# Weaving two kinds of recurrent chains into projections: fixed waits against an estimate of the engines' queues

## The chip, the cores and the metric

The kernel runs on one core of a Trainium2 chip. The core has a matmul engine (PE), a vector engine (DVE), an activation engine (ACT), a general engine (POOL), and a queue (SP) that starts transfers. Each takes its instructions in the order in which they stand in its queue. The metric is the device time of one launch in microseconds (us), the median of several runs.

## The reference, cut to what matters

One layer of a decoder with 2048 prompt tokens, 16 meta tokens and 8 short sample sequences of 4 tokens. The normalised tokens go through one input projection. Four heads are retention heads, four are gated delta-rule heads; both are recurrences over chunks of 128 tokens. Then come the output projection, a norm, a dense feed-forward part and a second norm.

```python
proj = h @ w_in
# retention, per chunk c of 128 tokens
scores = (q @ k.T) * decay
out    = scores @ v + q_d @ s
s      = gamma**C * s + k_d.T @ v
# gated delta rule, per chunk
lower  = strict_tril(k @ k.T * decay) * beta
w_v, w_k = solve(I + lower, [v * beta, k * beta * gam])
u      = w_v - w_k @ s
out    = q_g @ s + (q @ k.T * decay) @ u
s      = cd * s + k_t.T @ u
# after either: out = rms_norm(out) * silu(gate)
y = layer_norm(alpha * h + concat(out_r, out_g) @ w_out);  y = layer_norm(alpha * y + swiglu(y))
```

## The kernel before

**Stages.** The first stage, `attention`, takes the tokens in four blocks of four chunks (block 0 has a fifth, short tile with the sample and meta tokens). `attn_block` goes through the eight heads of a block in the order of `order(b)`, retention (r) and delta rule (g) mixed: r0 g0 r1 g1 r2 g2 r3 g3, and in the last block r0 g0 g1 r1 g2 g3 r2 r3. The second stage is the output projection and the feed-forward part; it is not touched.

**Projections.** `ret_proj` and `gdn_proj` compute a head's projections. float32 operands are split in two float32r parts, so each product is three matmuls (`mm3`, line 288). The results go to PSUM tiles `pj`. The weights arrive by transfer as `raw` and are split into `wh` (ACT, line 237) and `wl` (DVE, line 244). In `ret_proj` DVE writes `qk` and `rotB` (lines 439 and 440, the rotary step) and `rg` (line 456). Both functions are generators: `mm3g` yields after each few products.

**Chains.** When a head's projections are written, its chain is started, and runs beside the projections of the heads after it. `ret_chain` is the retention: `flip` (turn q and k), `score`, `mix` for each chunk, then the norm, and a turn of each output (line 563, `rt` from `rv`). `gdn_chain` runs `gdn_group` for the four chunks of a block together (and in block 0 a second, small group for the short tile). Its steps are: decays E by `mg` (line 788); turned values and keys, `vb` (805, 806) and `kT` (810, 812); the products kT x kT (816); LT, the masked product (818); the inverse of I + LT by block doubling, which starts with the factors `Z` and `U` (827, 828), then `T` (834, products of U with the unit matrix), six levels in which `w` from `T` and `Lm` gives `Z` (840, 842) and `w` from `Z` and `U` gives the next T and U (847, 849); a refinement; and then the recurrence, chunk after chunk: products with the state S (902, 903), `r` (905), `u` (910, 911), and the new S and output V (919 to 922). `Lm`, the masks of the six levels, are six instructions on POOL (830). At the end come the sums of squares, a reciprocal square root by some twelve small DVE instructions on tiles `rqa`, `rqt`, `rqy` (lines 189 to 201), the multiplication of V by it (929, 931), four turns on PE (933, `sc` from `ident` and V), and a product with the gate (937). A delta-rule chain must be over before the next one starts (`start` calls `finish`).

**The order of the work.** The program is written by one Python loop: it takes the next piece of a projection, and then asks `advance` whether a chain may issue its next step. Before, each `yield` of a chain names a fixed wait out of a table (`LAT`, 17 numbers), times a factor (`SLACK`), and `advance` subtracts the projection work that has been written:

```
38   LAT = [1.0, 0.7, 0.7, 0.7, 2.0, 0.7, 0.5, 1.2, 1.8, 0.9, 1.0, 1.0, 1.7, 1.0, 0.6, 0.5, 0.5]
974      def advance(self, us):
975          for key in list(self.active):
976              c = self.active[key]
977              c[1] -= us
978              while c[1] <= 0:
979                  w = next(c[0], None)
980                  if w is None:
981                      del self.active[key]
982                      break
983                  c[1] += w * SLACK[key]
```

What is written is then ordered once more by a scheduler: it gives each engine's queue its order, and lets a ready instruction pass one that is not ready, earlier written ones first. So the order on the engines is read from the built program, not from the code alone.

Of the kernel before, what the change touches and what calls it, by code (L numbers as in the profile page):

```python
# [148 lines left out]
class _Cut:  # L149
    """Allocates [128, full, ...] tiles and hands out their first n rows of dim 1."""  # L150
# [13 lines left out]

class Builder:
    def __init__(self, tc, I, O):
        self.tc, self.nc, self.I, self.O = tc, tc.nc, I, O
        _, self.off, self.gam, _ = _consts()
        self.es = ExitStack()
# [13 lines left out]
    def rsqrt(self, x, n, rows, pool, scale, eps):  # L183
        """(scale x + eps)^-0.5; x may be a list of equal parts."""
# [19 lines left out]
    def layer_norm(self, src, rows, g, b, pool, fast=False, pinned=False):  # L204
        """LayerNorm of rows in place; src is the row, or its two halves. fast: the vector engine alone."""
# [42 lines left out]
    def load_piece(self, src, ab=False, ring=None, later=False, el="dve"):  # L248
        """2048 (+64) columns of weights as a pair of float32r parts."""
# [26 lines left out]
    def mm3g(self, out, lh, ll, rh, rl, kn, per):  # L276
        """As mm3, with a yield of the tensor engine's time after every few k."""
# [6 lines left out]
    def mm3(self, out, lh, ll, rh, rl, kn, first=True, last=True):  # L284
        """out (+)= sum_k l(k)^T r(k), with float32 operands in two float32r parts."""
# [55 lines left out]
    def phase_ln(self, b):  # L341
        """Embedding LayerNorm of the tokens of block b, a tile at a time."""
# [11 lines left out]
    def first_block(self):  # L354
        """As phase_ln and turned for the first block, whose tokens and weights are loaded together."""
# [38 lines left out]
    def phase_t(self, b, tiles, x=None):  # L394
        """Transposes of normalised rows, one tile of tokens at a time."""
# [14 lines left out]
    def next_piece(self):  # L410
        """The weights whose turn it is; the load of those after them starts."""
        w = self.ahead
        while self.pend:
            self.split(*self.pend.pop(0))
        self.age = 0
        self.ahead = self.load_piece(*self.todo.pop(0), later=True) if self.todo else None
        return w

    def ret_proj(self, b, h, gates, out, before=None):
# [39 lines left out]
        if before and b == 0:  # L459
            # the weights come before the tokens: each tile of these meets all of those  # L460
# [20 lines left out]
    def ret_chain(self, b, h, qkvg, mixd):  # L481
        """The retention itself; yields the time until its next products can start."""
# [62 lines left out]

        flip(0)
        yield LAT[0]
        for t in range(n):
            score(t)
            yield LAT[1]  # L550
            if t + 1 < n:
                flip(t + 1)
                yield LAT[2]
            mix(t)
            yield LAT[3]
        rs = self.rsqrt(ss[:, :n], n, 128, self.sm, 4.0 / HD, 4.0 * RMS_EPS)
        yield LAT[4]
        for t, (rows, c0, ch) in enumerate(tiles):
            orow = NS if ch < 0 else 128
            o = oc[t]  # L560
            nc.vector.scalar_tensor_tensor(out=o, in0=o, scalar=rs[:orow, t:t + 1], in1=vg[t][1][:orow], op0=ALU.mult, op1=ALU.mult)
            p = self.prt.tile([128, 128], F32, tag="rt", name="rt")[:, :orow]
# [5 lines left out]
            yield LAT[5]  # L568
# [3 lines left out]
    def state_out(self, kt, u, S0, cd, gam, out):  # L572
        """out_b = decay_b S0_b + kt_b^T u_b for the eight sample sequences."""
# [82 lines left out]
    def gdn_proj(self, b, h, G, out):  # L656
# [15 lines left out]
        def flip(a):  # L672
            """Token-major q or k: sums of squares, and k itself."""
# [73 lines left out]
    def gdn_chain(self, b, h, cvz, G, mixd):  # L747
        """The gated delta rule itself; yields as ret_chain does."""
# [16 lines left out]
    def gdn_group(self, b, h, cv, zg, sk, kp, G, mixd, ts, tiles):  # L765
        """One group of chunks; yields where the tensor engine has to wait for another one."""
# [16 lines left out]
        # decays exp(G_i - G_j) as [j, i]  # L783
# [466 lines left out]
```

## Time and profile before

| | |
|---|---|
| device time, median of 3 runs | 3137.73 us (3137.69 to 3143.98) |
| the profiled execution: from its first to its last instruction | 3141.4 us |
| PE busy | 2994.8 us, 95% |
| DVE busy | 1826.4 us, 58% |
| ACT, POOL busy | 967.1 us, 565.9 us |
| end of the first stage | about 1366 us |

In a row of the profile, the line number is that of the code before; `pj<-wh,xT` names the tile written and the tiles read. A matmul with float32 operands is recorded as two. "Idle" ahead of an instruction is put down to what it waited for last. The granted clock is PE's clock as a share of full speed.

### The profile page before, as it was taken

How to read it: one execution, taken by the hardware profiler on the slowest of the kernel's cores; microseconds unless marked ns; L12 is line 12 of the kernel's file. 1: busy time of each engine (PE TensorE's matmuls, PEld its weight loads, DVE VectorE, ACT ScalarE, POOL GpSimd, SP SyncE). 2: the span in 40 equal slices, each digit the busy share in tenths (PEclk: the TensorE clock that was granted, in tenths of full speed). 3: DMA queues.
4: the chain of work that ended last, by engine and by line, in shares of the span. 5: the costliest groups of instructions: out<-in, count | busy, mean ns of one | idle time of the engine just before them, and what ended most of it. 6: DMA issues, size and time to landing. Idle time of an engine off the chain costs nothing. (4 is left out here: it accounts for less than half of the span.)

```text
span 3141.4 us, 44842 instructions
## 1 busy us (share of the span) xinstructions
PE 2994.8 (95%) x17858; PEld 2593.6 (83%) x17858; DVE 1826.4 (58%) x4024; ACT 967.1 (31%) x2179; POOL 565.9 (18%) x570
## 2 busy tenths in 40 slices
PE   7999998999999988999999999999999999999997
PEld 6988887888888877878999999998777877878787
DVE  7777777877787777767333333333684343333346
ACT  2434443545544545433111111111233111111111
POOL 1332222221222122202100001110131000001002
PEclk9999998999999999999999999999999999999999
DMA  5222222222222111152111111112242111111111
GB/s 198 85 75 79 95 99 79 88 93 88 78 93 97 59 53 66 48 180 64 54 41 54 41 41 54 41 41 68 71 145 81 41 54 41 54 41 54 40 41 54
DMA packets 91986, 225.28 MB, mean 72 GB/s; under 512 B 10960, under 2 KB 39168, under 8 KB 91776
## 3 DMA queue, kind: packets, MB, share of 16 engines
q1 hardware_dynamic: 91776, 222.41, 21.5%
q8 instruction: 140, 2.29, 0.3%
q14 instruction: 70, 0.57, 0.1%
HBM read 191.87 MB, written 30.51 MB: 71 GB/s over the span
## 5 line engine op out<-in xcount | busy, mean ns | idle before, releaser
L288 PE MATMUL g<-fxT,wh 128*128 128x352 f32 (+2 forms) x3648 | 954.9, 344 | 1.5 <-DVE th L1110 0.6
L288 PEld LDWEIGHTS g<-fxT,wh 128*128 128x128 f32 x3648 | 646.6, 188 | 62.8 <-ACT fxT L237 1.0
L288 PE MATMUL d<-wh,ff 128*128 128x512 f32 (+1 forms) x1912 | 618.3, 397 | 15.8 <-DVE y L1129 6.9
L288 PE MATMUL g<-fxT,wl 128*128 128x352 f32 (+2 forms) x1824 | 626.9, 344 | 0.0
L237 ACT CAST wh<-raw 128x1024 fp32r<-128x1024 f32 x276 | 285.4, 1050 | 637.9 <-PE d L288 407.5
L288 PE MATMUL pj<-wh,xT 128*128 128x256 f32 (+2 forms) x2176 | 458.0, 298 | 14.5 <-DVE rotB L440 8.1
L288 PEld LDWEIGHTS d<-wh,ff 128*128 128x128 f32 (+1 forms) x1912 | 351.1, 184 | 116.5 <-DVE y L1129 16.8
L244 DVE TENSOR_TENSOR wl<-raw,wh 128x1024 fp32r<-128x1024 f32 x274 | 356.5, 1313 | 56.5 <-ACT wh L237 54.8
L288 PE MATMUL pj<-xT,wh 128*128 128x512 f32 (+1 forms) x1280 | 380.3, 379 | 0.8 <-DVE kp L685 0.6
L288 PE MATMUL d<-wl,ff 128*128 128x512 f32 (+1 forms) x956 | 377.9, 395 | 1.7 <-DVE wl L244 1.7
L244 POOL TENSOR_TENSOR ff<-th,ff 128x352 fp32r<-128x352 f32 (+2 forms) x114 | 142.7, 1251 | 1299.7 <-ACT ff L237 1254.8
L288 PEld LDWEIGHTS pj<-wh,xT 128*128 128x128 f32 (+1 forms) x2176 | 357.8, 193 | 20.3 <-issue 8.6
L288 PEld LDWEIGHTS g<-fxT,wl 128*128 128x128 f32 x1824 | 342.4, 188 | 28.8
L1129 DVE TENSOR_TENSOR y<-y,d 128x512 f32<-128x512 f32 (+1 forms) x340 | 231.6, 685 | 187.3 <-PE d L288 187.1
L288 PE MATMUL pj<-wl,xT 128*128 128x256 f32 (+2 forms) x1088 | 319.3, 294 | 0.5 <-POOL wl L244 0.5
L1110 DVE SCALAR_TENSOR_TENSOR th<-th,g 128x352 f32<-128x352 f32 (+2 forms) x114 | 65.2, 572 | 338.3 <-ACT th L1109 338.3
L1111 DVE SCALAR_TENSOR_TENSOR th<-th,g 128x352 f32<-128x352 f32 (+2 forms) x114 | 65.2, 572 | 336.9 <-PE g L288 336.7
L288 PE MATMUL pj<-xT,wl 128*128 128x512 f32 (+1 forms) x640 | 230.1, 360 | 0.0
L288 PEld LDWEIGHTS pj<-xT,wh 128*128 128x128 f32 x1280 | 209.0, 192 | 19.4 <-DVE S L584 3.0
L288 PEld LDWEIGHTS d<-wl,ff 128*128 128x128 f32 (+1 forms) x956 | 175.7, 184 | 44.9 <-DVE wl L244 2.7
L288 PEld LDWEIGHTS pj<-wl,xT 128*128 128x128 f32 (+1 forms) x1088 | 210.4, 193 | 1.1 <-POOL wl L244 0.8
L1109 ACT ACTIVATE th<-g 128x352 f32<-128x352 f32 (+2 forms) x114 | 57.7, 506 | 371.8 <-PE g L288 343.0
(272 smaller groups left out, 3812.6 us busy)
## 6 DMA issues: line engine op xcount, KB each, us to landing
raw<-gu SPq DMA_DIRECT2D x88, 512.0 KB, 3.9
raw<-wret SPq DMA_DIRECT2D x64, 512.0 KB, 4.0
raw<-wgd SPq DMA_DIRECT2D x64, 512.0 KB, 3.9
raw<-dn SPq DMA_DIRECT2D x44, 512.0 KB, 3.9
raw<-wout SPq DMA_DIRECT2D x16, 512.0 KB, 4.2
ff<-mixd SPq DMA_DIRECT2D x16, 512.0 KB, 4.1
y<-xhat SPq DMA_DIRECT2D x16, 512.0 KB, 4.8
out_y<-y SPq DMA_DIRECT2D x16, 512.0 KB, 2.6
```

Of the source, the lines that this page charges most:

```text
L237: i = nc.scalar.copy(out=h, in_=src)
L244: i = (nc.vector if el == "dve" else nc.gpsimd).tensor_tensor(out=l, in0=src, in1=h.bitcast(F32), op=ALU.subtract)
L288: self.nc.tensor.matmul(out, lhsT=a(k), rhs=b(k), start=first and k == 0 and i == 0, stop=last and k == kn - 1 and i == 2)
L1109: nc.scalar.activation(out=t, in_=ps[0], func=AF.Tanh, scale=0.5)
L1110: nc.vector.scalar_tensor_tensor(out=t, in0=t, scalar=1.0, in1=ps[0], op0=ALU.add, op1=ALU.mult)
L1111: nc.vector.scalar_tensor_tensor(out=t, in0=t, scalar=0.5, in1=ps[1], op0=ALU.mult, op1=ALU.mult)
L1129: nc.vector.tensor_tensor(out=ys, in0=ys, in1=p, op=ALU.add)
```

## The change

The fixed waits are gone. While the program is written, a `Meter` keeps for each engine the time until which its written instructions would keep it busy, and for each tile the time at which it would be written; `Ring` does so for the PSUM pools' buffers, and `Timed` wraps every engine so that each instruction is noted. A chain now yields what its next step needs (tiles, or a pool from which it takes a buffer), and `advance` issues the step when all of it is expected 0.35 us or more before PE's written work ends. `finish`, with no projection work left, sets PE's time forward to the next expected step. One wait is new: ahead of the turns of the finished V (line 933 of before); and one in the recurrence has moved ahead of the products with S. The rest of the diff takes comments out. All instructions now come from one line (262, in `Timed`).

```diff
-SLACK = {"r": 1.0, "g": 1.8}
+MARGIN = 0.35
-LAT = [1.0, 0.7, 0.7, 0.7, 2.0, 0.7, 0.5, 1.2, 1.8, 0.9, 1.0, 1.0, 1.7, 1.0, 0.6, 0.5, 0.5]
+class Meter:
+    BASE = {"vector": (0.17, 0.00088), "scalar": (0.19, 0.00078), "gpsimd": (0.12, 0.0025)}
+    HOP = 0.12
+    def when(self, need):
+        return max([0.0] + [n.next_free() if isinstance(n, Ring) else self.made.get(self.name(n), (0.0, 0))[0] + self.HOP for n in need])
+    def took(self, engine, op, out, kw):
...
+        if engine == "tensor":
+            dt = kw["rhs"].dtype if op == "matmul" else kw["lhs"].dtype
+            if dt == F32R:
+                return n * 1.09 / 2400 + 0.002
+            if dt == F16:
+                return n / 2400 + 0.0025
+            return (4 if op == "matmul" else 2) * (n / 2400 + 0.0025)
...
+        a, b = self.BASE[engine]
+        if op == "bn_stats":
+            n = 512
+        return a + b * n + (0.2 if kw.get("accum_out") is not None else 0.0)
+    def note(self, engine, op, args, kw):
...
+        t = self.free[engine]
+        for a in ins:
+            end, by = self.made.get(self.name(a), (0.0, engine))
+            t = max(t, end + (0.0 if by == engine else self.HOP))
+        o = self.name(out)
+        t = max(t, self.used.get(o, 0.0) if engine == "tensor" else 0.0)
+        end = t + self.took(engine, op, out, kw)
+        self.free[engine] = end
...
-    def advance(self, us):
+    def advance(self):
         for key in list(self.active):
-            c = self.active[key]
-            c[1] -= us
-            while c[1] <= 0:
-                w = next(c[0], None)
-                if w is None:
+            while key in self.active:
+                c = self.active[key]
+                if self.m.when(c[1]) > self.m.free["tensor"] - MARGIN:
+                    break
+                need = next(c[0], None)
+                if need is None:
                     del self.active[key]
-                    break
-                c[1] += w * SLACK[key]
+                else:
+                    c[1] = need
     def finish(self, key):
         while key in self.active:
-            self.advance(0.3)
+            self.advance()
+            if key in self.active:
+                t = min(self.m.when(c[1]) for c in self.active.values()) + MARGIN
+                self.m.free["tensor"] = max(self.m.free["tensor"], t)
...
-        yield LAT[9]
+        yield U, self.pw
         pt = wide()[:R, :m, :R]
...
-            yield LAT[10]
+            yield T, Lm, self.pw
...
-            yield LAT[11]
+            yield Z, U, self.pw
...
+            yield S, kT, self.psc, self.pw
             pp = self.psc.tile([128, 4, 128], F32, tag="sc", name="sc")
...
-            yield LAT[14]
             nc.vector.scalar_tensor_tensor(out=r[:orow], in0=pp[:orow, 0, :], scalar=gc("ng", i, orow), in1=vb[:orow, i, :], op0=ALU.mult, op1=ALU.add)
...
+            yield r, V
             nc.tensor.matmul(pp[:R, 2, :], lhsT=V[:, i, :], rhs=r, start=True, stop=True)
             nc.scalar.copy(out=u, in_=pp[:R, 2, :])
-            yield LAT[15]
+            yield u, kt, AT
...
-            yield LAT[16]
         rs = self.rsqrt(ss[:orow], m, orow, self.sm, 1.0 / HD, RMS_EPS)
         nc.vector.tensor_tensor(out=rs, in0=rs, in1=cq[:orow], op=ALU.mult)
+        nc.vector.tensor_tensor(out=O[:orow], in0=O[:orow], in1=rs.unsqueeze(2).broadcast_to([orow, m, 128]), op=ALU.mult)
+        yield O, self.psc
         p = self.psc.tile([128, 4, 128], F32, tag="sc", name="sc")[:, :m, :orow]
-        nc.vector.tensor_tensor(out=O[:orow], in0=O[:orow], in1=rs.unsqueeze(2).broadcast_to([orow, m, 128]), op=ALU.mult)
```

What it moves is shown at the place where a delta-rule chain ends and the next one begins. First DVE before, in block 1 between the second and the third head: from the next chain's LT to the finished output V_8073.

```order
L818 TENSOR_TENSOR LT<-w,mg 128x512
L200 SCALAR_TENSOR_TENSOR rqt<-rqt,rqa 128x4
L827 TENSOR_TENSOR Z<-LT,lvl 128x512
L201 SCALAR_TENSOR_TENSOR rqy<-rqt,rqy 128x4
L439 TENSOR_TENSOR qk<-pj,rott 128x256
L929 TENSOR_TENSOR rqy<-rqy,gsk 128x4
L828 SCALAR_TENSOR_TENSOR U<-Z,ident 128x512
L931 TENSOR_TENSOR V_8073<-V_8073,rqy 128x512
```

The next chain's U and the finished V follow each other. DVE at the same place in the changed program, from U to the finished output, which is V_8143 there:

```order
L262 SCALAR_TENSOR_TENSOR U<-Z,ident 128x512
L262 SCALAR_TENSOR_TENSOR rqy<-rqt,rqy 128x4
L262 TENSOR_TENSOR wl<-raw,wh 128x1024
L262 TENSOR_TENSOR rqt<-rqy 128x4
L262 TENSOR_TENSOR rotB<-pj,rott 128x256
L262 SCALAR_TENSOR_TENSOR rqt<-rqt,rqa 128x4
L262 SCALAR_TENSOR_TENSOR Z<-w,ident 128x512
L262 SCALAR_TENSOR_TENSOR rqy<-rqt,rqy 128x4
L262 TENSOR_TENSOR wl<-raw,wh 128x1024
L262 TENSOR_TENSOR rqy<-rqy,gsk 128x4
L262 SCALAR_TENSOR_TENSOR rg<-rg,rv 128x128
L262 TENSOR_TENSOR V_8143<-V_8143,rqy 128x512
```

U has moved ahead of the end of the old chain's norm; ten rows now stand between it and V, two splits of weights among them. PE before, at the same place: the last product of U, and the turns of V.

```order
L834 LDWEIGHTS U
L834 MATMUL w<-identh,U 128x128
L288 MATMUL pj<-wl,xT 128x256
L288 MATMUL pj<-wh,xT 128x256 x2
L933 MATMUL sc<-ident,V_8073 128x128 x4
```

Three projection products stand between them. PE in the changed program, from the last product of U:

```order
L262 MATMUL w<-identh,U 128x128
L262 MATMUL pj<-wh,xT 128x256
L262 MATMUL rt<-ident,qk 128x128 x4
L262 LDWEIGHTS Lm
L262 MATMUL w<-T,Lm 128x128
```

The next chain's first level (`w` from `T` and `Lm`) comes one projection product and four turns behind U; the turns of V_8143 have moved behind 27 more projection products. Third, DVE in block 0, between the first and the second head, before: the last rows of the old chain's norm.

```order
L440 TENSOR_TENSOR rotB<-pj,rott 128x256
L200 SCALAR_TENSOR_TENSOR rqt<-rqt,rqa 128x4
L900 COPY r<-vb 48x128
L201 SCALAR_TENSOR_TENSOR rqy<-rqt,rqy 128x4
L199 TENSOR_TENSOR rqt<-rqy 128x4
L200 SCALAR_TENSOR_TENSOR rqt<-rqt,rqa 128x4
L201 SCALAR_TENSOR_TENSOR rqy<-rqt,rqy 128x4
L929 TENSOR_TENSOR rqy<-rqy,gsk 128x4
L931 TENSOR_TENSOR V_2491<-V_2491,rqy 128x512
L937 SCALAR_TENSOR_TENSOR Uf<-sc,gwh,zg 128x512
L818 TENSOR_TENSOR LT<-w,mg 128x512
```

LT of the next chain comes behind V. DVE there in the changed program:

```order
L262 TENSOR_TENSOR rotB<-pj,rott 128x256
L262 SCALAR_TENSOR_TENSOR rqy<-rqt,rqy 128x4
L262 SCALAR_TENSOR_TENSOR U<-Z,ident 128x512
L262 TENSOR_TENSOR rqt<-rqy 128x4
L262 TENSOR_TENSOR LT<-w,mg 48x48
L262 SCALAR_TENSOR_TENSOR rqt<-rqt,rqa 128x4
L262 COPY r<-vb 48x128
L262 SCALAR_TENSOR_TENSOR rqy<-rqt,rqy 128x4
L262 TENSOR_TENSOR Z<-LT,lvl 48x48
L262 TENSOR_TENSOR rqy<-rqy,gsk 128x4
L262 SCALAR_TENSOR_TENSOR U<-Z,ident 48x48
L262 TENSOR_TENSOR V_2491<-V_2491,rqy 128x512
```

U of the main group (LT and Z ahead of it, not shown) and LT, Z, U of the small group have moved ahead of V.

More of the change, by code (lines that the diff above doesn't have):

```diff
@@ new lines, with __init__, next_free, tile @@
+class Ring:
+    of = {}
+    def __init__(self, pool, bufs, meter):
+        self.pool, self.bufs, self.meter = pool, bufs, meter
+        self.busy, self.at = [0.0] * bufs, 0
+    def next_free(self):
+        return self.busy[self.at % self.bufs]
+    def tile(self, *a, **kw):
+        t = self.pool.tile(*a, **kw)
+        i = self.at % self.bufs
+        self.at += 1
+        n = self.meter.name(t)
+        self.meter.used[n] = self.busy[i]
+        Ring.of[n] = self, i
+        return t
+class Timed:
+    def __init__(self, engine, key, meter):
+        self.engine, self.key, self.meter = engine, key, meter
+    def __getattr__(self, op):
+        f = getattr(self.engine, op)
+        def issue(*a, **kw):
+            i = f(*a, **kw)
+            self.meter.note(self.key, op, a, kw)
+            return i
+        return issue
@@ L165, with __init__ @@
+class Engines:
+    def __init__(self, nc, meter):
+        for k in ("tensor", "vector", "scalar", "gpsimd", "sync"):
+            setattr(self, k, Timed(getattr(nc, k), k, meter))
 class Builder:
     def __init__(self, tc, I, O):
-        self.tc, self.nc, self.I, self.O = tc, tc.nc, I, O
+        self.m = Meter()
+        Ring.of = {}
+        self.tc, self.nc, self.I, self.O = tc, Engines(tc.nc, self.m), I, O
         _, self.off, self.gam, _ = _consts()
@@ L950, in attention @@
             self.mp = self.pool("mix", bufs=2, es=es)
-            self.pj = self.pool("p_pj", bufs=2, space=PSUM, es=es)
-            self.pw = self.pool("p_w", bufs=3, space=PSUM, es=es)
-            self.psc = self.pool("p_sc", bufs=1, space=PSUM, es=es)
-            self.prt = self.pool("p_rt", bufs=2, space=PSUM, es=es)
+            self.pj = Ring(self.pool("p_pj", bufs=2, space=PSUM, es=es), 2, self.m)
+            self.pw = Ring(self.pool("p_w", bufs=3, space=PSUM, es=es), 3, self.m)
+            self.psc = Ring(self.pool("p_sc", bufs=1, space=PSUM, es=es), 1, self.m)
+            self.prt = Ring(self.pool("p_rt", bufs=2, space=PSUM, es=es), 2, self.m)
             self.todo, self.pend = [], []
@@ L963, in attention @@
                 self.attn_block(b)
-            while self.active:
-                self.advance(0.3)
+            for key in ("r", "g"):
+                self.finish(key)
             nc.sync.dma_start(out=self.O["conv"], in_=self.cout)
```

58 lines of the change are left out of this document (44 added, 14 removed).

## The prediction

> **What bounds the kernel now.** I read the page first, then the windows, then the waits of the matmul engine, then its timeline and that of the vector engine at one place where the wait is long.
>
> ```profile
> span 3141.4 us, 44842 instructions
> PE 2994.8 (95%) x17858; PEld 2593.6 (83%) x17858; DVE 1826.4 (58%) x4024; ACT 967.1 (31%) x2179; POOL 565.9 (18%) x570
> ```
>
> The matmul engine (PE) is busy for 95% of the span, so the kernel is as long as PE's work plus PE's gaps. The same instructions are issued before and after the change (4024 on DVE and 570 on POOL in both), so only the gaps, and the clock, can move.
>
> ```profile
> 0.00:25.00 25.00, 9.30 (x43) 7.61 (x44) 19.39 (x69) 5.19 (x8) 5.71 (x13) 0.91 0.70 242
> 25.00:1366.00 1341.00, 1249.48 (x9125) 1097.95 (x9124) 1020.88 (x2592) 626.60 (x1700) 326.99 (x377) 0.97 0.26 84
> 665.60:672.20 6.60, 6.28 (x32) 5.90 (x33) 4.15 (x7) 0.59 (x1) 6.08 (x6) 0.50 0.11 42
> ```
>
> The columns are the stretch, its length, then busy time of PE, weight loads, DVE, ACT and POOL, the granted clock, and DMA. The change touches only the stage from about 0 to 1366 us (projections and chains). In it PE idles 1341 - 1249 = 92 us, and the clock is 0.97 on average, which is 0.03 x 1341 = 40 us of lost clock. DVE is busy 1021 of 1341 us (76%); no other engine comes near. The third row is a stretch behind one gap, at half clock.
>
> ```profile
> PE w L834 <- DVE U L828: 23.2, 14, 3.5
> PE sc L933 <- DVE V L931: 17.1, 14, 3.1
> PE pj L288 <- DVE rotB L440: 8.1, 5, 3.1
> PE sc L910 <- DVE r L905: 5.8, 7, 1.3
> PE pt L406 <- DVE rqy L201: 4.6, 2, 2.3
> PE rt L563 <- DVE rv L561: 4.4, 4, 1.9
> ```
>
> These are PE's waits from 27 to 1366 us: total, times, longest. All are on DVE. U and V alone make 40.3 us, 14 times each. There are 16 delta-rule chains (4 heads in 4 blocks), so 15 places where one ends and the next begins, which I call hand-overs; both waits sit there. U is the first factor of the new chain's inverse; V (at L931) is the finished output of the old chain, multiplied by its norm, which PE turns at L933. One hand-over, on PE and then on DVE:
>
> ```profile
> 653.40 0.38 PE L919 MATMUL sc<-u,kt 128*128 128x128 f32 x2
> 653.62 0.39 PE L921 MATMUL w<-u,E 128*128 128x128 f32 x2
> 654.26 0.63 PE L810 MATMUL w<-ident,kp 128*128 128x128 f32 x4
> 654.64 0.36 PE L288 MATMUL pj<-wh,xT 128*128 128x256 f32 x1
> 658.25 1.05 PE L816 MATMUL w<-kT 128*128 128x128 f32 x8
> 659.05 0.36 PE L288 MATMUL pj<-wh,xT 128*128 128x256 f32 x1
> 661.71 0.28 PE L288 MATMUL pj<-wl,xT 128*128 128x256 f32 x1
> 661.83 0.40 PE L288 MATMUL pj<-wh,xT 128*128 128x256 f32 x2
> 665.71 0.61 PE L834 MATMUL w<-identh,U 128*128 128x128 f16 x4 [3.48 <-DVE U L828]
> 667.27 1.12 PE L933 MATMUL sc<-ident,V 128*128 128x128 f32 x4 [0.21 <-DVE V L931]
> ```
>
> ```profile
> 654.89 0.34 DVE L922 SCALAR_TENSOR_TENSOR V<-qs,eg,w 128x128 f32<-128x128 f32 x1
> 662.82 1.11 DVE L201 SCALAR_TENSOR_TENSOR rqy<-rqt,rqy 128x4 f32<-128x4 f32 x1
> 664.97 0.68 DVE L828 SCALAR_TENSOR_TENSOR U<-Z,ident 128x512 f16<-128x512 f16 x1
> 665.57 1.64 DVE L931 TENSOR_TENSOR V<-V,rqy 128x512 f32<-128x512 f32 x1
> ```
>
> The old chain's last product (L921) ends at 653.84 (its start plus the 0.22 from L919 to L921). PE then has 8.2 us of other work, until 662.07, and idles 3.5 us. DVE takes the last output at 654.89 and ends U at 665.65, 10.8 us later, with a full queue. So DVE's queue sets the gap: it has more to do between these points than PE. The clock is at half from 665.6 (the window above).
>
> The Trainium skill, "TensorE: Matmul & The Clock Gate", section "Why this matters for your kernels", says that a PE gap of more than about 3 us drops the clock to half; by that rule the trace agrees here (3.48 us, then 0.50).
>
> **The change, part by part.** No instruction is added or removed; the estimate runs while the program is written. What moves is the order on the queues, in three ways.
>
> First, the hand-over. In the new order the factor of the next chain (LT, Z, U) stands nearer to the end of the old chain, and the finished V further from it. The prices, all from DVE's groups in this stage:
>
> ```profile
> L244 DVE TENSOR_TENSOR wl<-raw,wh 128x1024 fp32r<-128x1024 f32 x130 | 162.0, 1252 | 13.5 <-ACT wh L237 13.0
> L842 DVE SCALAR_TENSOR_TENSOR Z<-w,ident 128x512 f16<-128x512 f32 (+1 forms) x108 | 68.3, 632 | 54.6 <-PE w L840 53.9
> L201 DVE SCALAR_TENSOR_TENSOR rqy<-rqt,rqy 128x4 f32<-128x4 f32 (+5 forms) x153 | 40.4, 264 | 2.5
> L199 DVE TENSOR_TENSOR rqt<-rqy 128x4 f32<-128x4 f32 (+5 forms) x153 | 37.7, 247 | 2.6
> L200 DVE SCALAR_TENSOR_TENSOR rqt<-rqt,rqa 128x4 f32<-128x4 f32 (+5 forms) x153 | 33.8, 221 | 2.6
> L440 DVE TENSOR_TENSOR rotB<-pj,rott 128x256 f32<-128x256 f32 (+1 forms) x68 | 28.0, 411 | 0.0
> L889 DVE TENSOR_SCALAR kt<-kp,eg 128x128 f32<-128x128 f32 (+1 forms) x68 | 27.5, 408 | 0.2
> L456 DVE SCALAR_TENSOR_TENSOR rg<-rg,rv 128x128 f32<-128x128 f32 (+1 forms) x68 | 26.3, 387 | 38.3 <-ACT rg L455 38.3
> L502 DVE TENSOR_SCALAR rkd<-qk,cb 128x128 f32<-128x128 f32 (+1 forms) x67 | 20.6, 307 | 2.0 <-POOL qk L441 2.0
> L931 DVE TENSOR_TENSOR V<-V,rqy 128x512 f32<-128x512 f32 (+1 forms) x20 | 17.4, 868 | 0.2
> L806 DVE TENSOR_TENSOR vb<-w,sv 128x512 f32<-128x512 f32 (+1 forms) x20 | 12.0, 599 | 2.9 <-PE w L805 2.9
> L929 DVE TENSOR_TENSOR rqy<-rqy,gsk 128x4 f32<-128x4 f32 (+1 forms) x20 | 6.4, 320 | 0.3
> ```
>
> At the hand-over shown, the new order has on DVE, from the old chain's last output to U, one wl, one kt, two rkd, two L201, one L199, one L200 and the L929 less, and one vb more: 1.25 + 0.41 + 0.61 + 0.53 + 0.25 + 0.22 + 0.32 - 0.60 = 2.99 us, less the 0.07 us by which rows on DVE overlap (654.89 + 0.34 runs into the next row), for eight rows net: 2.4 us. So U comes 10.8 - 2.4 = 8.4 us after the last output. PE has there, counted in the new order, 38 projection products of 0.12 (661.71 to 661.83), the four L816 products in 0.8 (658.25 to 659.05), and two sets of four turns in 0.4 each (654.26 to 654.64): 6.2 us instead of 8.2. U's lateness is then 2.2 us where the same account gave 2.6 (the measured 3.5 contains 0.9 by which DVE began late). Gain: 0.4 us.
>
> From U to V the old order has only V's own row on DVE, the new one eleven (second piece of the order): 0.26 + 1.25 + 0.25 + 0.41 + 0.22 + 0.63 + 0.26 + 1.25 + 0.32 + 0.39 + 0.87 = 6.1, less eleven overlaps of 0.07: 5.3 us. PE has 28 projection products (3.4 us) and some 0.9 us of small ones between: 4.3 us. So V adds 1.0 us of lateness, where the old order showed 0.21. This hand-over loses about 0.4 us.
>
> I counted all 15 in the same way, rows of the order times group means, as DVE's work less PE's work from the old chain's last product, the larger of U's and V's. Before and after, in us: block 0, 1.2 and 4.6, 1.2 and 4.6, 1.1 and 4.9; into block 1, 1.8 and 1.6; block 1, 2.0 and 2.3, 2.0 and 2.3, 1.6 and 4.3; into block 2, 2.0 and 1.6; block 2 as block 1; into block 3, 1.0 and 2.3; block 3, 2.0 and 3.5, 1.2 and 2.0, 2.0 and 3.3. The sums (before rounding) are 24.9 before and 46.2 after: **+21.3 us**. The large terms are block 0, where the new chain's LT, Z and U of both its groups are put ahead of V (third piece of the order). Both ends of this price: the waits of U, V and r measured 23.2 + 17.1 + 5.8 = 46.1 us where I count 24.9, a ratio of 1.85; at that ratio it is +39. Below, if V's rows run beside gaps that PE has anyway, it is what U gains, 15 x -0.4 = -6. I take +21.3, because it comes from the rows themselves.
>
> Second, the recurrence and the retention chain. A step is now issued only when its operands and its PSUM buffer are expected. At the retention's last turn (rt from rv) the projection work between cause and use rises from a median of 5.8 to 7.8 us over 64 steps in the order: most of that row's 4.4 us should go, -3. In the recurrence fewer small rows stand between S and r: of 5.8 us I take -2. Bounds: 0 and -10. The inner steps of the inverse (Z, 96 of them) stand as far apart as before (medians 2.1 and 2.1 us): 0, covered by projection products; were that cover gone, each would cost DVE's 0.63 us.
>
> Third, what costs nothing: the new wait ahead of the turned V only delays the issue of four turns, behind which in PE's queue stand projection products, whose cost is in the count above. The waits for rotB (8.1) are for a PSUM buffer behind the same DVE queue and stay. The 25 us of start and the time after 1366 us are untouched; the last chains end under the output projection, as before. SP issues the same transfers, and no wait of PE in the list is for a DMA.
>
> Sum: +21.3 - 3 - 2 = **+16.3 us**. The profiled execution has a span of 3141.4 us, so 3157.7 for a profile like it; the median of the runs shown, 3137.73, is 3.7 below the span, so 3154.
>
> **The rivals.**
>
> *The blocked vector rows (slower still).* While POOL writes the six Lm of a new chain, small DVE rows wait:
>
> ```profile
> L830 POOL TENSOR_TENSOR Lm<-LT,lvl 128x512 f16<-128x512 f32 (+1 forms) x108 | 141.2, 1339 | 36.6 <-DVE LT L818 22.1 <-DVE rqt L200 9.4 <-DVE rqy L201 3.7
> ```
>
> The row L201 at 662.82 took 1.11 us against a mean of 0.26, and V 1.64 against 0.87. Six Lm last 8.0 us, from LT on. Before, V is through in 5 us of that; in the new order V stands about 8 us behind LT, so all six can block a row ahead of it. Against it: the means already hold an average share. With the ratio 1.85 the time is 3137.7 + 39 - 5 = 3172.
>
> The Trainium skill, "SBUF — State Buffer", section "Who interferes with whom", says that a DVE instruction with two SBUF inputs and a GpSimd instruction that reads SBUF exclude each other for a whole instruction. By that rule four more rows would be blocked at each hand-over; at the 0.8 us of the two rows above, the sum would be 15 x 4 x 0.8 = 48 us more, near this rival; the two slow rows agree with it.
>
> *Shorter gaps free the clock (faster).* U's gap splits into one before U and one before V. At the hand-over shown 3.48 us becomes about 3.1 (3.48 - 0.4) and 1.0. If gaps so cut no longer bring the half clock, half of the 40 us of lost clock returns (-20), and U's gaps give 14 x 0.5 = -7: 3137.7 - 27 = 3111. It decides at the gap before U: the 0.50 window followed 3.48 us, and the kernel has longest gaps of 3.1 (V, rotB). Against it: 3.1 is not much less, and block 0's new gaps are longer.
>
> By the Trainium skill's rule of about 3 us ("TensorE: Matmul & The Clock Gate", as above) most of the cut gaps would be too short, which speaks for this rival and against my sum.
>
> *Nothing moves.* The program's order is made again by the scheduler, which lets ready instructions pass. For it: equal medians in Z. Against it: the pieces of the order. It gives 3138.
>
> **How the numbers follow.** My forecast, 3154, has a chance of 0.38; the blocked rows 0.17; nothing moves 0.17; shorter gaps 0.28. A change of 0.2% (6.3 us) is about what a measurement of this kernel can tell, so slower is 0.38 + 0.17 = 0.55, the same 0.17, faster 0.28. The forecast's own range is 3144 to 3164: 5 us each way by the bounds of the second part, and as much again if each of the 15 counts is off by a third of a us. The range for all cases goes from 3106, a little below the clock rival, to 3188: the blocked rows' 3172 with a third of the 48 us on top.
>
> **What would show it.** After, all recorded lines are one helper's, so tiles tell: the wait of sc for V should rise from 17.1 to 30 to 45 us, that of w for U stay at 18 to 24, that of rt for rv fall below 2. DVE's rows from LT to V should take about 8 us instead of 5 in the middle blocks. The granted clock before 1366 us should stay at 0.96 to 0.97; at 0.98 or more the clock rival is right. If V's waits do not rise, my count is wrong where it takes DVE as never idle between the last output and V.

## The result, and the profile after

The changed kernel is slower: median 3194.77 us (3192.72 to 3198.06) against 3137.71; ratio 1.0179, 95% interval 1.0165 to 1.0193. That is 57 us where 16 were forecast: the direction was right, the time lies 7 us above the range. The views show one execution each, of the kernel before one whose span, 3141.4 us, lies above its median, and of the changed kernel the shortest (3192.72). The two spans differ by 49.5 us, and the rows below account for that much, not for all 57.

The page of the changed kernel, its head and engines:

```profile
span 3190.9 us, 44848 instructions
PE 3026.3 (95%) x17858; PEld 2622.2 (82%) x17858; DVE 1851.4 (58%) x4024; ACT 972.4 (30%) x2179; POOL 582.5 (18%) x570
```

Each engine's count of instructions is that of before, and yet PE is busy for 31.5 us more (2994.8 before). The first stage ends at 1417 us, so its row in the table of windows (stretch, length, then PE, weight loads, DVE, ACT, POOL, clock, DMA) is this:

```profile
25.00:1417.00 1392.00, 1283.12 (x9123) 1128.16 (x9122) 1045.49 (x2592) 631.73 (x1699) 344.61 (x377) 0.94 0.25 81
```

Against the 1341 us of before the stage is 51 us longer. PE idles 1392 - 1283.1 = 108.9 us instead of 91.5: 17.4 more. The other 33.6 us are PE's own products (1283.1 against 1249.5, 9123 records against 9125), at a mean clock of 0.94 instead of 0.97. In the trace's record of the clock, which is 1.0 or 0.5, half clock lasts 160.4 us up to 1450 us, in 27 stretches; before, 95.6 us in 17. Half of the 64.8 us more is 32.4 us of lost clock, close to the 33.6.

The waits of PE from 27 to 1417 us (total, times, longest):

```profile
PE sc L262 <- DVE V L262: 25.1, 13, 5.3
PE w L262 <- DVE U L262: 23.0, 12, 4.2
PE sc L262 <- DVE r L262: 8.1, 8, 1.4
PE pj L262 <- DVE wl L262: 6.7, 8, 2.3
PE pj L262 <- DVE rotB L262: 6.1, 3, 3.1
```

V costs 8.0 us more than before (17.1), U as much (23.2), r 2.3 more, and wl, which was not on the list, 6.7. The hand-over that the prediction went through, on PE and then on DVE:

```profile
698.22 0.40 PE L262 MATMUL w<-identh,U 128*128 128x128 f16 x4 [2.58 <-DVE U L262]
698.63 0.60 PE L262 MATMUL rt<-ident,qk 128*128 128x128 f32 x4
699.29 0.38 PE L262 MATMUL w<-T,Lm 128*128 128x128 f16 x4
700.39 0.58 PE L262 MATMUL pj<-wl,xT 128*128 128x256 f32 x1 [0.72 <-DVE wl L262]
...
706.32 0.66 PE L262 MATMUL sc<-ident,V 128*128 128x128 f32 x4
```

```profile
694.01 0.68 DVE L262 TENSOR_TENSOR LT<-w,mg 128x512 f32<-128x512 f32 x1
...
695.34 1.11 DVE L262 TENSOR_TENSOR rqt<-rqy 128x4 f32<-128x4 f32 x1
...
696.71 0.86 DVE L262 SCALAR_TENSOR_TENSOR rqt<-rqt,rqa 128x4 f32<-128x4 f32 x1
697.48 0.68 DVE L262 SCALAR_TENSOR_TENSOR U<-Z,ident 128x512 f16<-128x512 f16 x1
698.09 1.12 DVE L262 SCALAR_TENSOR_TENSOR rqy<-rqt,rqy 128x4 f32<-128x4 f32 x1
699.13 1.21 DVE L262 TENSOR_TENSOR wl<-raw,wh 128x1024 fp32r<-128x1024 f32 x1
700.26 1.11 DVE L262 TENSOR_TENSOR rqt<-rqy 128x4 f32<-128x4 f32 x1
...
705.49 0.68 DVE L262 TENSOR_TENSOR V<-V,rqy 128x512 f32<-128x512 f32 x1
```

The masks `Lm` on POOL at that time, then LT at the same place before, then a stretch of the changed kernel behind U's gap, as in the table of windows:

```profile
694.77 8.82 POOL L262 TENSOR_TENSOR Lm<-LT,lvl 128x512 f16<-128x512 f32 x6 [1.91 <-DVE rqy L262]
```

```profile
661.49 0.69 DVE L818 TENSOR_TENSOR LT<-w,mg 128x512 f32<-128x512 f32 x1
```

```profile
699.70:706.40 6.70, 6.01 (x28) 6.01 (x29) 6.47 (x10) 2.76 (x6) 5.65 (x4) 0.50 0.51 157
```

U's gap fell from 3.48 to 2.58 us, but half clock follows all the same. From LT to the end of V DVE now takes 12.2 us (694.01 to 706.17; before, 5.7: from 661.49 to 667.21). V ends that late and PE does not wait for it: at half clock its products last until then. So the lateness that was forecast as a wait for V stands here as slow products: at full clock those from 700.39 on, 5.9 us, would have taken about half as long (an estimate), and PE would have waited some 3 us for V instead.

### The profile page after: what moved, and what is told of

Its sections match the earlier page's. It is cut to its first block, busy times and chain, and to the rows that moved or that the text cites. A ratio compares the mean times of both kernels' runs of the same rounds, so it can differ in the third digit from the quotient of the medians.

```text
span 3190.9 us, 44848 instructions
## 1 busy us (share of the span) xinstructions
PE 3026.3 (95%) x17858; PEld 2622.2 (82%) x17858; DVE 1851.4 (58%) x4024; ACT 972.4 (30%) x2179; POOL 582.5 (18%) x570
## 5 line engine op out<-in xcount | busy, mean ns | idle before, releaser
L262 PE MATMUL pj<-wh,xT 128*128 128x256 f32 (+2 forms) x2176 | 466.1, 302 | 14.5 <-DVE rotB L262 6.1
L262 DVE TENSOR_TENSOR wl<-raw,wh 128x1024 fp32r<-128x1024 f32 x274 | 364.3, 1342 | 58.8 <-ACT wh L262 56.9
L262 PE MATMUL pj<-xT,wh 128*128 128x512 f32 (+1 forms) x1280 | 366.8, 372 | 0.6 <-DVE zg L262 0.5
L262 PE MATMUL pj<-wl,xT 128*128 128x256 f32 (+2 forms) x1088 | 327.1, 301 | 7.3 <-DVE wl L262 6.7
L262 PEld LDWEIGHTS pj<-xT,wh 128*128 128x128 f32 x1280 | 217.6, 192 | 26.4 <-issue 2.3
L262 POOL TENSOR_TENSOR Lm<-LT,lvl 128x512 f16<-128x512 f32 (+1 forms) x108 | 148.3, 1405 | 32.2 <-DVE rqy L262 17.6
```

The source lines that it names most:

```text
L262: i = f(*a, **kw)
```

## The experiments

Times by ratio to the kernel before on the same chip; half clock from the trace's record, up to 1450 us; U and V are PE's waits for them in us, from 25 to 1430 us (e3b, e7, e10 and e11 to 1450). The last two columns are of the one profiled execution; in e2 and e12 that was the longest of all (3173.0 and 3136.8 us).

| kernel | median us | ratio (95%) | half clock us | U, V |
|---|---|---|---|---|
| before | 3137.7 | 1 | 95.6 | 23.2, 17.1 |
| after | 3194.8 | 1.0179 (1.0165 to 1.0193) | 160.4 | 23.0, 25.1 |
| e1, after with dummy products | 3193.0 | 1.0175 (1.0161 to 1.0190) | 75.1 | 6.7, 25.0 |
| e2, before with dummy products | 3164.0 | 1.0085 (1.0070 to 1.0100) | 81.9 | 10.2, 23.3 |
| e3, retention alone | 3173.3 | 1.0117 (1.0104 to 1.0130) | 102.4 | 17.2, 28.5 |
| e3b, the same, other end | 3173.1 | 1.0104 (1.0087 to 1.0120) | 116.1 | 19.0, 27.4 |
| e4, delta rule alone | 3178.1 | 1.0125 (1.0110 to 1.0139) | 126.3 | 19.3, 27.9 |
| e5, without the new wait | 3188.9 | 1.0158 (1.0144 to 1.0171) | 146.8 | 23.0, 25.4 |
| e6, one step per piece | 3210.6 | 1.0223 (1.0206 to 1.0241) | 174.1 | 25.3, 43.6 |
| e7, MARGIN 1.5 | 3230.7 | 1.0298 (1.0283 to 1.0314) | 158.9 | 12.4, 57.5 |
| e9, ending one chain only | 3205.9 | 1.0204 (1.0187 to 1.0221) | 174.1 | 27.9, 32.3 |
| e10, MARGIN -0.5 | 3200.2 | 1.0203 (1.0188 to 1.0218) | 136.5 | 30.4, 19.5 |
| e11, MARGIN -1.5 | 3280.8 | 1.0456 (1.0438 to 1.0474) | 187.7 | 12.8, 18.9 |
| e13, after, padded rows | 3184.5 | 1.0149 (1.0133 to 1.0164) | 129.7 | 22.7, 26.6 |
| e16, after, less on DVE | 3159.9 | 1.0065 (1.0051 to 1.0079) | 102.4 | 16.0, 17.4 |
| e15, after, both | 3144.6 | 1.0015 (1.0006 to 1.0025) | 54.6 | 15.9, 18.2 |
| e12, before, less on DVE | 3127.3 | 0.9963 (0.9952 to 0.9975) | 88.7 | 15.5, 17.7 |
| e14, before, both | 3123.6 | 0.9948 (0.9933 to 0.9962) | 64.9 | 12.6, 18.0 |
| e17, before, both, V's row on DVE | 3118.9 | 0.9936 (0.9923 to 0.9948) | 51.2 | 8.5, 20.4 |

**What brings half clock (e8).** Before and after, the stretches of half clock up to 1450 us are 3.41, 6.83, 10.24 or 13.65 us long, and all begin on one grid of 3.41 us. That suggested a share: for each window of the grid I summed the columns that PE streamed at full speed, times the rows used over 128 (a float32 record counts its columns twice). Before and after, all 44 windows of full clock that were followed by half clock had a share of 0.43 or less (43 of them 0.41 or less), and none of those that were followed by full clock was under 0.39. Five of the 27 falls of the changed kernel have no wait of 0.5 us in the window ahead of them, but products with 32 or 48 rows for 1.3 to 3.4 us of it. Without the weight by rows, five of the 27 have shares of 0.48 to 0.83. A kernel of nothing but float16 products, with zeros as operands, tested it:

```diff
+            def dense(rows, n, cols=128):
+                p = ps.tile([128, 512], F32, tag="p", name=f"r{rows}c{cols}_")
+                for _ in range(n):
+                    nc.tensor.matmul(p[:cols], lhsT=w[:rows, :cols], rhs=x[:rows], start=True, stop=True)
+            def spaced(widths, n):
...
+                for _ in range(n):
+                    for q in widths:
+                        nc.tensor.matmul(p[:, :q], lhsT=w, rhs=y[:, :q], start=True, stop=True)
+                    nc.scalar.copy(out=y, in_=p)
```

> Not the layer: nothing of the reference is computed; only stretches of products. First dense ones of 512 columns with 128, 96, 64, 56, 52, 48, 44 and 32 rows (then 128 rows with 48 and 32 columns of weights), each followed by dense ones with 128 rows; then stretches of 512, 768, 1024, 1280, 1536, 2048 and 2560 columns and a wait of about 1 us for a copy by the activation engine after each. Share theory (the clock of a 3.4 us window falls when streaming, weighted by the rows used, filled less than about 0.38 of the window before): half clock for dense 48 rows (0.375) or fewer, none for 52 rows (0.41) or more, none for few columns of weights; with waits of 1 us half clock up to 768 to 1024 columns (share 0.24 to 0.45) and none from 1280 on. Gap theory (only a gap of about 3 us brings half clock): no half clock in any of these stretches.

Five windows, in this order: dense products with 52 rows, with 48 rows, with 128 rows and 32 columns of weights; then 1280 columns and a copy, and 1536 columns and a copy. The clock is the third number from the end:

```profile
270.00:307.00 37.00, 37.00 (x174) 16.09 (x172) 0.00 (x0) 0.00 (x0) 0.00 (x0) 1.00 0.00 1
342.00:406.00 64.00, 64.00 (x152) 22.24 (x150) 0.00 (x0) 0.00 (x0) 0.00 (x0) 0.50 0.00 0
702.00:739.00 37.00, 37.00 (x173) 16.60 (x172) 0.00 (x0) 0.00 (x0) 0.00 (x0) 1.00 0.00 0
1000.00:1050.00 50.00, 31.15 (x77) 10.09 (x76) 0.00 (x0) 15.19 (x26) 0.00 (x0) 0.50 0.00 0
1080.00:1126.00 46.00, 24.24 (x90) 8.61 (x90) 0.00 (x0) 17.49 (x30) 0.00 (x0) 1.00 0.00 0
```

```profile
991.62 0.70 PE L1371 MATMUL s__3715<-y,wt 128*128 128x512 f16 x3 [0.67 <-ACT y L1372]
993.05 0.70 PE L1371 MATMUL s__3715<-y,wt 128*128 128x512 f16 x3 [0.73 <-ACT y L1372]
...
1090.79 0.81 PE L1371 MATMUL s__3967<-y,wt 128*128 128x512 f16 x3 [0.73 <-ACT y L1372]
1092.33 0.81 PE L1371 MATMUL s__3967<-y,wt 128*128 128x512 f16 x3 [0.73 <-ACT y L1372]
```

With 48 rows (a share of 48/128 = 0.375) PE is never idle and runs at half clock; with 52 rows (0.41) at full clock. Few columns of weights change nothing. With waits of 0.7 us, 1280 columns every 1.43 us (0.217 us for 512 of them, so 0.54 / 1.43 = 0.38) fell to half clock, 1536 every 1.54 us (0.65 / 1.54 = 0.42) did not. No gap in these stretches comes near 3 us. So the share decides, here with a limit between 0.38 and 0.41, and the gap theory fell; only the place of the limit among the spaced stretches was expected a step lower.

**Does it cost the time? (e13)** The 32 products `pj` from `ub` have 32 rows. Padded with zeros to 128 they take as many columns:

```diff
-        ub = self.ax.tile([128, NB, 128], F32, tag="xa", name="ub")[:NS]
+        ubz = self.ax.tile([128, NB, 128], F32, tag="xa", name="ub")
+        ktz = mp.tile([128, 128], F32, tag="rkd", name="ktz")
+        nc.gpsimd.memset(ubz, 0.0)
+        nc.gpsimd.memset(ktz, 0.0)
+        nc.scalar.copy(out=ktz[:NS], in_=kt)
+        ub = ubz[:NS]
...
-            nc.tensor.matmul(p, lhsT=kt, rhs=ub[:, 4 * i:4 * i + 4, :].rearrange("p a e -> p (a e)"), start=True, stop=True)
+            nc.tensor.matmul(p, lhsT=ktz, rhs=ubz[:, 4 * i:4 * i + 4, :].rearrange("p a e -> p (a e)"), start=True, stop=True)
```

> The changed kernel with the 32 products of 32 rows by 512 columns (pj from ub) padded with zeros to 128 rows; same products, same columns, 8 zeroings on the general engine and 8 small copies more. Share theory (rows count): the half clock around these products (75 to 85, 198 to 208, 307, 413 us of the changed kernel, some 30 us) goes, 10 to 15 us lost come back: 3178 to 3188. If rows do not count: 3193 to 3203.

Around two of these products, the changed kernel first, then the padded one:

```profile
75.00:85.20 10.20, 10.20 (x32) 6.87 (x31) 5.46 (x13) 3.27 (x8) 0.52 (x3) 0.50 0.27 78
412.90:419.70 6.80, 6.80 (x30) 6.05 (x29) 5.59 (x19) 1.53 (x5) 0.00 (x0) 0.50 0.68 222
```

```profile
75.00:85.20 10.20, 10.20 (x61) 8.50 (x60) 5.74 (x13) 4.00 (x13) 1.02 (x5) 0.85 0.29 104
401.40:408.20 6.80, 5.08 (x36) 3.95 (x36) 6.80 (x25) 2.57 (x6) 0.95 (x1) 1.00 0.73 234
```

The second rows of both begin 1.5 us after the first of four such products. The changed kernel is at half clock in both places with PE busy throughout; with more rows the clock is 0.85 and 1.00. Some 10 us come back (3184.5, ratios 1.0179 and 1.0149; the two intervals just miss each other), at the lower edge of what the share theory expected, although the program does more: its trace has 16 zeroings on POOL, not the 8 that were expected, and 8 copies on ACT.

**Dummy products (e1, e2).** Eight float16 products of 512 columns into the tile that the turns of U and of V overwrite, in the 16 large groups:

```diff
+    def fill(self, t, n):
+        for _ in range(n):
+            self.tc.nc.tensor.matmul(t, lhsT=self.identh, rhs=self.lvl[:, 0:4, :], start=True, stop=True)
```

> Clock theory: of the 49.5 us that the new order adds to the span, about 32 are half clock (47.8 us lost before, 80.2 after, up to 1450 us) and some 12 are waits. The clock of a 3.4 us window falls to half when PE streamed for less than about 0.38 of the window before it. Eight products of 0.21 us (1.7 us) written into the PSUM tile just ahead of the turns of U and of the finished V, in the 16 large groups, fill the wait without shortening it. Some 35 of the lost us should come back, at most 54 us of dummy products less 48 us of waits (6 to 15 us) are paid: 3165 to 3180. Queue theory (only the late vector rows cost, the clock is a small part): the waits end when they ended, and the dummies that lie outside a wait cost: 3195 to 3210.

> The same fill in the kernel before, whose waits for U and V are 40 us. Clock theory: about 51 us stand at half clock behind these two waits, 25 us lost; most of it returns, the dummies cost 54 less 40 us at the most: 3115 to 3140. Queue theory: 3138 to 3155.

All four forecasts missed. One reason is that the second scheduler put most of the dummies elsewhere; in e2 only nine of U's 16 sets of eight stand right ahead of U's turns. In e1, at the hand-over shown above, those for U stand at 692.2, and U's turns at 698.7:

```profile
692.22 1.89 PE L1093 MATMUL w<-lvl,identh 128*128 128x512 f16 x8
```

What the pair still tells: half clock fell from 160.4 to 75.1 us in the changed kernel, and 54 us of added products (16 x 16 x 0.213) cost nothing (3193.0). But the 43 us of clock that came back (half of 85.3) did not make it faster either. In the kernel before it fell only from 95.6 to 81.9, and the same products cost 26 us.

**Which part of the change (e3, e3b, e4).** One chain by the estimate, the other by the fixed waits:

```diff
+            if key != METERED:
+                c[1] -= us
+                while c[1] <= 0:
...
+                    c[1] += w * SLACK[key]
+                continue
```

> Retention by the estimate, the delta rule by the fixed waits of before. If the hand-over of the delta-rule chains is the cause, 3130 to 3145 with V's wait near 17 us. If retention steps issued in clumps are the cause, over 3160.

> The delta rule by the estimate, retention by the fixed waits. If the hand-over of the delta-rule chains is the cause, 3180 to 3200, half clock near 80 us lost; if retention is, 3135 to 3150.

> e3_ret_only again, with the last chains ended in steps of 0.3 us by turns, as before, since some 20 of its 35 us came after the last projection product, from how they were ended. If the two parts of the change add up (the delta rule alone cost 40 of 57): 3148 to 3158. If retention by the estimate is itself as dear as e3 showed: 3168 to 3175.

The delta rule alone costs 40 us, 2 us below the range that was forecast for it. Retention, forecast at nothing (and then at 10 to 20), costs 33 to 37 by itself, with V's wait at 28.5 instead of 17, and ending the last chains as before made no difference; so the second readings of e3 and e3b held in their numbers, and what makes retention dear is not shown. By the times of the projections' products in the traces, e3 was 12 and e3b 20 us late at the last one, and the rest came behind it, where the changed kernel loses nothing; why is open. The two do not add up to 57. Nor is it half clock in the main: e4 has 30.7 us more of it than before and e3 6.8, of which half is lost, 15 and 3 us.

**Where the lateness comes from (e5, e6, e7, e9, e10, e11).** I had three ideas. The first: the new wait ahead of V's turns delays V.

```diff
-        yield O, self.psc
```

> The changed kernel without the one new wait (on the finished V, ahead of its turns). Hand-over theory as in the prediction (V is late because its rows stand behind the next chain's): the rows are written at once with the end of the chain, V's wait falls from 25 to 17 us or less, 3170 to 3185. If the wait is only where the lateness shows, and the rows of the norm are written at the same place as before: 3190 to 3200.

It gave 6 us by the ratios, whose intervals overlap, 1 us under the second forecast, and V's wait stayed (25.4). So the new wait is where the lateness shows, not its cause. The second: chain steps that are left when a head's projections are used up are issued with nothing beside them. MARGIN sets how many; counted while the program is written, they hold 132 us of products in the changed kernel, 93 before.

> MARGIN 1.5 instead of 0.35: each chain step is issued later. Counted while the program is written, the products that a chain still has to issue when its head's projections are used up (in finish, with no projection beside them) are 93 us before, 132 us after, 166 us here. Left-over theory (these bare stretches cost the waits and the half clock): slower than after by 30 to 50 us, 3225 to 3245. Hand-over theory (V late on the vector engine behind the next chain's rows): later steps give the vector engine more time: 3175 to 3195.

> MARGIN -0.5: each step is issued half a us before the estimate has it ready. Left over without projections: 43 us. Left-over theory: most of the 57 us comes back, 3130 to 3160, half clock down to some 50 us lost or less. Hand-over theory: no better than after, 3185 to 3215, since the next chain's rows only move further ahead of V.

> MARGIN -1.5: left over without projections 7 us. Left-over theory: 3100 to 3150, if the waits that each too early step brings (0.6 us for a row of the inverse, over 200 steps, less what the second scheduler lets pass) stay under 30 us. Hand-over theory: 3195 or more.

```profile
PE sc L262 <- DVE V L262: 57.5, 15, 6.4
PE w L262 <- DVE U L262: 12.4, 9, 4.8
```

```profile
PE w L262 <- DVE U L262: 30.4, 15, 6.3
PE sc L262 <- DVE V L262: 19.5, 10, 9.7
```

The first two rows are MARGIN 1.5, the last two -0.5. The idea was right at 1.5 (3231) and wrong at -0.5 and -1.5 (43 and 7 us left over), where the time is no shorter than at 0.35. The hand-over reading missed at 1.5 and held at the other two in its numbers, so neither reading carries all three. Between 1.5 and -0.5 the margin moves the wait from V to U. Third: clumps, by ending one chain at a time, or by one step per piece.

```diff
-    def advance(self):
-        for key in list(self.active):
+    def advance(self, only=None):
+        for key in [only] if only else list(self.active):
...
-            self.advance()
+            self.advance(key)
...
-                t = min(self.m.when(c[1]) for c in self.active.values()) + MARGIN
+                t = self.m.when(self.active[key][1]) + MARGIN
```

```diff
                 else:
                     c[1] = need
+                    break
```

> The changed kernel, but when a chain has to be ended without projections, only that chain is advanced; the retention chain keeps its steps for the projections that follow. In the middle blocks 16 steps are issued there now (7 before the change), half of them the retention's. If these bare steps cost: 3175 to 3187. If they hide in the chain's own waits: 3190 to 3200.

> The changed kernel with at most one step of each chain after one piece of a projection. If steps issued together make the bare stretches (chain work alone for 1 us or more: 306 us, 224 before the change): stretches shorter, 3175 to 3188. If the stretches come from the ends of the heads (132 us of products there, 136 in this kernel): 3193 to 3203.

By the ratios both are slower than the changed kernel, by 8 us (e9, intervals overlap) and 14 us (e6), above both forecasts of each; the reading that such bare steps cost fell with both, and V's wait grew (32.3 and 43.6).

**DVE's load at the hand-over (e12, e16, e15, e14, e17).** The premise of the prediction: DVE's queue sets the gaps. Then rows taken off DVE there must shorten them.

```diff
-            nc.vector.tensor_scalar(out=kt, in0=kp[:, i, :], scalar1=gc("et", i), scalar2=None, op0=ALU.mult)
+            nc.scalar.activation(out=kt, in_=kp[:, i, :], func=AF.Copy, scale=gc("et", i))
...
-        nc.vector.tensor_tensor(out=vb, in0=p, in1=lane(G["sv"][:R, here, h]), op=ALU.mult)
+        for i in range(m):
+            nc.scalar.activation(out=vb[:, i, :], in_=p[:, i, :], func=AF.Copy, scale=gc("sv", i))
...
-        nc.vector.tensor_tensor(out=O[:orow], in0=O[:orow], in1=rs.unsqueeze(2).broadcast_to([orow, m, 128]), op=ALU.mult)
+        for i in range(m):
+            nc.scalar.activation(out=O[:orow, i, :], in_=O[:orow, i, :], func=AF.Copy, scale=rs[:, i:i + 1])
```

> The kernel before, with kt, vb and the norm's multiplication of V moved from the vector engine to the activation engine (four copies with a scale for each row of vb and V). If the vector engine's queue sets the gaps at the hand-over: it loses 0.41 (one kt) and 0.60 (vb) ahead of U and 0.87 ahead of V, so U and V wait 15 to 25 us less, and with the half clock behind them 3100 to 3125. If the activation engine's copies are late instead (four of 0.25 us in a row): 3135 to 3150.

> The changed kernel with kt, vb and the norm's multiplication on the activation engine, rows not padded. Padding alone gave 10 us, both 50. If the two add, the load gives 40: 3150 to 3160, and half clock falls with the waits, from 80 to about 40 us lost. If padding matters more once the waits are short (windows near the limit): 3162 to 3175.

> The same two edits in the changed kernel, whose estimate sees the moved rows. If its waits are the vector engine's at the hand-over, as before the change: 10 us for the rows and 12 to 25 us for the load, 3160 to 3173. If the order that the estimate makes is the cause whatever the load: 3175 to 3185.

> The kernel before with both edits that gained: kt, vb and the norm's multiplication on the activation engine (gained 12 us) and the padded rows (gained 10 us in the changed kernel; before, some 17 us of half clock stand around those products, 5 to 8 us lost). If the gains add: 3115 to 3124. If the 8 zeroings on the general engine or the ring of tiles delay the chains more than the clock gives: 3126 to 3135.

> The best kernel so far (3123.6 us) with the norm's multiplication of V back on the vector engine. V's wait was 17 us there before and 18 us on the activation engine, so the move may have given nothing: then 3118 to 3126. If the 0.87 us row on the vector engine delays the next chain's rows: 3127 to 3135.

The changed kernel's small rows of the norm on DVE from 25 to 1420 us, and below them the same with both edits (e15; count, then busy us and mean ns):

```profile
L262 DVE SCALAR_TENSOR_TENSOR rqt<-rqt,rqa 128x4 f32<-128x4 f32 (+5 forms) x153 | 48.6, 317 | 2.1
L262 DVE TENSOR_TENSOR rqt<-rqy 128x4 f32<-128x4 f32 (+5 forms) x153 | 47.2, 308 | 2.5
L262 DVE TENSOR_TENSOR rqy<-rqy,gsk 128x4 f32<-128x4 f32 (+1 forms) x20 | 13.1, 657 | 0.2
```

```profile
L262 DVE SCALAR_TENSOR_TENSOR rqt<-rqt,rqa 128x4 f32<-128x4 f32 (+5 forms) x156 | 25.8, 166 | 3.1
L262 DVE TENSOR_TENSOR rqt<-rqy 128x4 f32<-128x4 f32 (+5 forms) x156 | 29.1, 186 | 3.2
L262 DVE TENSOR_TENSOR rqy<-rqy,gsk 128x4 f32<-128x4 f32 (+1 forms) x20 | 3.1, 153 | 0.3
```

In the kernel before the moved rows give 12 us (e12), a little less than expected; in the changed one 35 (e16, the upper end of what was expected if the parts add), where the waits for U and V fall from 48.1 to 33.4. The rows suggest why it is more there. Of the norm's rows of 128 by 4 (L199, L200, L201), counted in the traces, 22 of 252 ran beside an `Lm` of POOL before, at a mean of 1025 ns, the others at 190. In the changed kernel it is 66 of 243, at 994 ns, the others at 181. With DVE relieved (e16, e15) it is none: the norm is over before the first `Lm`. So the new order pushed 44 more small rows into the time of the masks, at 0.81 us each 36 us of DVE at the hand-overs, where the masks are. The finished V's own row (128 by 512, both inputs in SBUF) ran beside an `Lm` 6 times of 16 before and 10 of 16 in the changed kernel, there at a mean of 1.43 us, the other six at 0.68. A row that reads PSUM kept its time: rotB from pj took 0.41 us on the mean 17 times beside an `Lm`, and as much the other 47 times. No run moved the masks alone, so how much of the 35 us is due to blocked rows is open. With both edits the changed kernel is 50 us faster than without (e15, below all forecasts) and its half clock falls from 160.4 to 54.6 us. Against the order of before with the same edits (e14) it still loses 1.0015 / 0.9948, 0.67% or 21 us. The old order gains 16 us by both edits, as expected if the gains add (e14). So some 35 of the 57 us hang on DVE's load at the hand-over and on the rows that PE uses; what the 21 us are is open.

The best kernel is the old order with kt and vb on ACT and padded rows, V's row on DVE (e17): 3118.9 us, 0.9936 (0.9923 to 0.9948), faster than the kernel before and the changed one, though its interval overlaps that of e14. Its stage:

```profile
25.00:1342.00 1317.00, 1229.43 (x9122) 1082.48 (x9122) 977.55 (x2504) 670.13 (x1843) 331.14 (x393) 0.98 0.26 85
```

PE's busy time is 20 us less than before (1249.5) at a clock of 0.98; its idle time, 87.6, only 3.9 less. Most of the gain is clock. Moving V's row to ACT gave nothing, as the first reading expected.

## Why the prediction was wrong

- **The time of PE itself.** "Only the gaps, and the clock, can move" was right, but the sum left the clock at its 0.97. It fell to 0.94, and 33.6 of the 51 us of the stage are PE's longer products, with 64.8 us more of half clock. This is the step that failed: a term of the sum that was set to nothing. The split says where the time stands, not what the clock would cost by itself. At the hand-over shown, slow products cover what would have been a wait for V; e1 had 85 us less half clock and was no faster; and e7 is 37 us slower than the changed kernel by the ratios with as much half clock, while its waits for U and V are 22 us longer together. So late rows of DVE can show as waits or as slow products, and no run separates the two costs.
- **The clock rival had the wrong sign.** It took a gap's length as what counts. U's gap fell as forecast (to 2.58; "about 3.1" was written), but behind it now stand four turns and the first level in float16, which stream little, then a wait of 0.72 for wl, and the windows stay under the share. The rule of "TensorE: Matmul & The Clock Gate" in the Trainium skill, "Why this matters for your kernels" (a gap of about 3 us), agreed at the one place the prediction looked at; the runs differ from it: 0.73 us waits or no gap at all do it too.
- **The hand-over, +21.3.** The order was read rightly: V late, block 0 worst (half clock up to 490 us went from 37.5 to 71.7 us by the clock's record; the waits for V of 3.34 and 5.31 us at 238 and 453 us are there). As waits, U, V and r rose by 10.1 (46.1 to 56.2), where some of the lateness is covered by slow products, as above. V's wait, 25.1, lies below the forecast 30 to 45; U's, 23.0, in the 18 to 24.
- **-3 and -2.** rt's wait for rv fell from 4.4 to 1.8, as forecast. r rose by 2.3 where 2 less was forecast. The 6.7 for wl was not foreseen.
- **Idle in sum.** 17.4 us more against 16.3 forecast: close, but by luck: the hand-over's waits rose by 10.1 instead of 21.3, and wl and r, which were not foreseen to rise, made up for part of it.
- **The blocked rows.** Their rival had a chance of 0.17 and was right in its mechanism: from LT to V 12.2 us where 8 were forecast, rows of 0.86 to 1.12 us beside `Lm`. The forecast priced these rows at means from the old order (0.22 to 0.26 us), where few of them stood beside `Lm`. By "SBUF — State Buffer", "Who interferes with whom", in the Trainium skill, a DVE instruction with two SBUF inputs and a GpSimd instruction that reads SBUF exclude each other; the prediction's estimate from it was four more rows at each hand-over, 60 at 0.8 us. The trace has 44 more at 0.81 (and L929, 320 ns before, 657 after), so it agrees in kind and roughly in size. Even so that rival's time, 3172, lacked the clock.
- **The change's own prices.** The estimate in the changed program makes the same error: it takes 0.17 us for such a small row (`BASE`, under The change), where they took 0.31 to 0.66 us on the mean, and full speed for PE. No run corrected these prices, so whether the estimate would then beat the fixed waits is open.

## What to carry to other kernels

Before reordering work on a matmul engine that is 95% busy, price each window of the clock, not only each gap: a window that streams under some 0.4 of its time, weighted by rows, makes the next one slow, whether by waiting or by products with few rows. A mean duration holds only for the order in which it was measured; rows that are moved beside another engine's work take a new price. And when an order is disputed, take load off the queue that sets the gaps: that gave 12 us in the old order and 35 in the new.

## What was not expected of the hardware

The clock goes by a grid of 3.41 us and by the share of it that PE streamed, with a limit between 0.38 and 0.41 in the kernel of nothing but products (one window of the layer fell at 0.43); rows count (48 of 128 without a pause: half clock; 52: full), columns of weights do not (32 of 128: full). The Trainium skill, "TensorE: Matmul & The Clock Gate", "What's actually happening", says that the window is of 3413 ns and runs freely; the trace agrees (stretches of 3.41, 6.83, 10.24 and 13.65 us, all on one grid).

Zeros can pay: padding 32 products from 32 to 128 rows, with 16 zeroings and 8 copies more, made the changed kernel 10 us faster.
